# A transformer block on one core: its head with one-column matmuls, column arithmetic on ScalarE, products ordered by pass

## The chip, the cores and the metric

The kernel runs on one core of a Trainium2 chip. Times are device microseconds (us) of one execution. The profile records one execution; its times count from the start of its span.

## The reference

One block of a transformer, for 256 tokens (S) of 1024 features (D), in float32. A vector `c` sets six columns of modulation. What matters here is the first part, up to the projection; all that follows (attention of 8 heads, a gating unit, a feed-forward of width 4096, a last norm) is the same before and after.

```
c_act = jax.nn.silu(c)
mod = (c_act @ w_ada[l] + b_ada[l])[:, None, :]
shift1, scale1, gate1, shift2, scale2, gate2 = jnp.split(mod, N_MOD, axis=-1)
h = rmsnorm(x, g_mix[l]) * (1 + scale1) + shift1
proj = h @ w_in[l]
q, k, v, u, vs, ga, gb = jnp.split(proj, splits, axis=-1)
...
x = x + gate2 * (jnp.square(jax.nn.relu(h @ w_ff1[l])) @ w_ff2[l])
return rmsnorm(x, g_final)
```

## The kernel before

Features lie on partitions, tokens in the row. Every product of two float32 matrices is made from three passes of `float32r`: an operand is split into a high part (a copy cast to `float32r`) and a low part (the rest), and the passes are high by high, high by low and low by high. For weights, ScalarE (ACT) makes the high part `whi`, and VectorE (DVE) the low part `wlo`. Weights come in chunks of 1 MB (`raw`, five buffers) through the queue of SyncE (SP), in the order in which they are used.

**The head** loads the constants and x, makes silu(c) and spreads it over all partitions (`cps` by eight matmuls with an identity matrix, copied to `csb`), squares x, adds the squares up on VectorE, and sums them over the features by two matmuls with one column of ones. GpSimd (POOL) raises the sums to the power of -0.5 (`rs`); two matmuls spread that over the partitions (`rp`), and x times it is `xn`. Its first feature tile is multiplied on VectorE, the seven others on GpSimd. A few matmuls on a tile of zeros (`idle`, the function `spin`) are put in between.

**Phase 1** is a loop `kt` over the eight tiles of 128 features of h. A step has one chunk of adaLN weights and one of the projection. VectorE takes two products with `csb` along the row (`dot`, written `junk` in the trace, 1024 elements each, with a sum that a read of the accumulator delivers), makes from them the columns `acol` (scale) and `bcol` (shift), then `hf` = acol * xn + bcol. ScalarE makes the same with rounding, `hh`; VectorE takes the difference, `hl`. Then TensorE (PE) runs 24 products of 256 columns (q and k) and 12 of 512 columns (v and vs) on the step, into eight banks that are summed over all eight steps.

The orders on TensorE, VectorE and ScalarE in head and phase 1 are those in which the code is written (`InOrder`, pinned). In a step, ScalarE's casts `w_hi` are written around `h_hi`, so that one half of a step's weights is cast ahead of its `hh`. After phase 1 a scheduler orders the instructions.

Of the kernel before, what the change touches and what calls it, by code (L numbers as in the profile page):

```python
# [16 lines left out]
P = 128  # L17
# [17 lines left out]
class InOrder:  # L35
    """An engine whose instructions are issued in the order in which they are traced."""
# [11 lines left out]
def block_kernel(ctx, tc, xT, cols, wsguT, bsgu, w_a1, w_1, w_a, w_m, w_f, out):  # L48
# [46 lines left out]
    DVE.memset(ones, 1.0)  # L95
    nhalf = const.tile([P, 2], F32, name="nhalf")
    DVE.memset(nhalf, -0.5)
# [10 lines left out]
    eps = const.tile([P, 1], F32, name="eps")  # L108
    DVE.memset(eps, EPS)

    def sums(o, sq, first, last):
# [4 lines left out]
    def rstd(o, n):  # L116
        ms = wk.tile([P, 2], F32, name="ms", tag="ms")
        ACT.activation(out=ms, in_=o[:, 0:2], func=AF.Identity, scale=1.0 / n, bias=eps)
        rs = wk.tile([P, 2], F32, name="rs", tag="rs")
        nc.gpsimd.tensor_tensor(out=rs, in0=ms, in1=nhalf, op=ALU.pow)  # L120
        return rs

    def spread(rs):
        """One value per token, tokens on partitions -> on every partition, tokens in the row."""
        rp = bank()
        for t in range(2):
            PE.matmul(out=rp[:, P * t:P * t + P], lhsT=rs[:, t:t + 1].broadcast_to([P, P]), rhs=ident,
                      start=t == 0, stop=True, skip_group_check=t == 1)
        return rp

# [1 line left out]
    c_col = cols_sb[:, C_COL:C_COL + KT]  # L132
    cs = const.tile([P, KT], F32, name="cs")
    ACT.activation(out=cs, in_=c_col, func=AF.Tanh, scale=0.5)
    DVE.scalar_tensor_tensor(out=cs, in0=cs, scalar=1.0, in1=c_col, op0=ALU.add, op1=ALU.mult)
    csb = const.tile([P, D], F32, name="csb")
# [5 lines left out]
    ss = bank()  # L142
    sqs = [act.tile([P, 2, S], F32, name="sq", tag=t) for t in ("q1", "q2", "o1", "o2")]
    for i in range(4):
        ACT.activation(out=sqs[i], in_=x_sb[:, 2 * i:2 * i + 2], func=AF.Square)
        if i:
            DVE.tensor_tensor(out=sqs[0], in0=sqs[0], in1=sqs[i], op=ALU.add)
    DVE.tensor_tensor(out=sqs[0][:, 0], in0=sqs[0][:, 0], in1=sqs[0][:, 1], op=ALU.add)
    sums(ss, sqs[0][:, 0], True, True)
    for i in range(2):  # L150
        ACT.copy(out=csb[:, 512 * i:512 * i + 512], in_=cps[i])
    spin(4)
    rs1 = rstd(ss, D)
    identb = const.tile([P, P], BF16, name="identb")
    mask = const.tile([P, 2, P], BF16, name="mask")

# [17 lines left out]
    def column(acc, part, kt):  # L174
# [3 lines left out]
        if part in (SCALE1, SCALE2):  # L178
            g = (G_MIX, G_FFN)[n]
            DVE.scalar_tensor_tensor(out=acol[:, n, at], in0=acc, scalar=cols_sb[:, g + kt:g + kt + 1],  # L180
                                     in1=pre[:, n, at], op0=ALU.mult, op1=ALU.add)
        elif part in (SHIFT1, SHIFT2):
            DVE.tensor_tensor(out=bcol[:, n, at], in0=acc, in1=b, op=ALU.add)
# [4 lines left out]
    # the middle's weight chunks, and the adaLN chunks that are used beside them  # L188
# [62 lines left out]
    hh = act.tile([P, KT, S], F32R, name="hh", tag="b1")  # L251
    hl = act.tile([P, KT, S], F32R, name="hl", tag="b2")
    rb1 = wk.tile([P, S], F32, name="rb1", tag="sqa", bufs=1)
    xn = act.tile([P, KT, S + 2], F32, name="xn", tag="b3")
    wsg = const.tile([P, 8, P], F32, name="wsg", tag="c4")
    bsg = const.tile([P, NP, P], F32, name="bsg")
    for kt in range(KT):
        if kt + 2 < KT:
            ada[kt + 2] = load(w_a1[kt + 2], 2 if kt + 2 == KT - 1 else 1)
            wraw[kt + 2] = load(w_1[kt + 2], 4 if kt + 2 == KT - 1 else 2)  # L260
        raw, w_raw = ada.pop(kt), wraw.pop(kt)
# [4 lines left out]
        wp = [slice(2048 // np_ * i, 2048 // np_ * (i + 1)) for i in range(np_)]  # L266

        def w_hi(i):
# [5 lines left out]
        def cols_ab():  # L274
            column(da, SCALE1, kt)
            column(db, SHIFT1, kt)

        def h_hi():
            a, b = acol[:, 0, kt:kt + 1], bcol[:, 0, kt:kt + 1]
            ACT.activation(out=hh[:, kt], in_=xn[:, kt, 0:S], func=AF.Identity, scale=a, bias=b)  # L280
            DVE.tensor_scalar(out=hf, in0=xn[:, kt, 0:S], scalar1=a, scalar2=b, op0=ALU.mult, op1=ALU.add)

        def h_lo():
            DVE.tensor_tensor(out=hl[:, kt], in0=hf, in1=hh[:, kt].bitcast(F32), op=ALU.subtract)

        da, db = dot(raw, 0), dot(raw, 1)
        if kt == 0:
            for i in range(3):
                w_hi(i)
            cols_ab()  # L290
            rp = spread(rs1)
            spin(4)
            DVE.tensor_tensor(out=xn[:, 0, 0:S], in0=x_sb[:, 0], in1=rp[:, 0:S], op=ALU.mult)
            h_hi()
            w_lo(0)
            ACT.copy(out=rb1, in_=rp[:, 0:S])
            for i in range(1, KT):
                nc.gpsimd.tensor_tensor(out=xn[:, i, 0:S], in0=x_sb[:, i], in1=rb1, op=ALU.mult)
            w_lo(1)
            h_lo()  # L300
            w_lo(2)
            w_hi(3)
            w_lo(3)
            qk_ps = [bank() for _ in range(4)]
            vv_ps = [[bank() for _ in range(2)] for _ in range(2)]
        else:
            w_hi(0)
            cols_ab()
            h_hi()
            w_lo(0)  # L310
            w_hi(1)
            h_lo()
# [4 lines left out]
        f, l = kt == 0, kt == KT - 1  # L317
        for ft in range(8):
            o = qk_ps[ft // 2][:, S * (ft % 2):S * (ft % 2) + S]
            w = slice(P * ft, P * ft + P)  # L320
            mm3(o, wh[:, w], wl[:, w], hh[:, kt], hl[:, kt], f and ft % 2 == 0, l,
                skip_group_check=ft % 2 == 1)
        for n in range(2):
            w = slice(1024 + 512 * n, 1536 + 512 * n)
            for t in range(2):
                tk = slice(P * t, P * t + P)
                o = vv_ps[n][t]
                PE.matmul(out=o, lhsT=hh[:, kt, tk], rhs=wh[:, w], start=f, stop=False)
                PE.matmul(out=o, lhsT=hl[:, kt, tk], rhs=wh[:, w], start=False, stop=False)
                PE.matmul(out=o, lhsT=hh[:, kt, tk], rhs=wl[:, w], start=False, stop=l)  # L330
# [36 lines left out]
    def wide(n, ah, al, nk, base=0):  # L367
        """Two tiles of features from one chunk, tokens in the row."""
# [46 lines left out]
    def attn_turn(pr):  # L415
        # transposed probabilities: [keys 0:128 x queries 0:256 | keys 128:256 x queries 128:256]
# [48 lines left out]
    A0, S0, TD, OD = 1, 5, 2, 3  # when attention and the gating unit start; lags of transposes and products  # L465
# [233 lines left out]
    for q, first, last in ((sq3[:, 0], True, False), (sq[:, 0], False, False), (sq[:, 1], False, True)):  # L699
        sums(ss3, q, first, last)  # L700
    for ft in range(4, KT):
        turn(ft)
    rs3 = rstd(ss3, D)
# [11 lines left out]
def _ko(w, cols):  # L715
    """[K, N] -> chunks [N/cols][128][K/128 * cols] with k in (ko, p)."""
# [42 lines left out]
```

## Time and profile before

| what | value |
|---|---|
| time, median of 3 runs | 376.34 us (376.22 to 376.67) |
| the profiled execution: span from first to last instruction | 374.8 us |
| TensorE busy | 358.4 us (96%), 2884 matmul records |
| VectorE busy | 266.4 us (71%) |
| ScalarE busy | 206.0 us (55%) |
| GpSimd busy | 15.4 us (4%) |
| moved by DMA | 89.34 MB, mean 238 GB/s |

The profiled execution has no separate time on record: its span is 374.8 us, and the median lies 1.5 us above it. A busy share is a mean over the span; what a change in the head is worth depends on which wait ends last there.

### The profile page before, as it was taken

Reading aid. Unit: us, or ns where it says so; the run is one execution under the profiler, and the core shown is the slowest. Engines: PE = TensorE matmul, PEld = TensorE weight load, DVE = VectorE, ACT = ScalarE, POOL = GpSimd, SP = SyncE. Lnnn points to the kernel's source line nnn. Section 1 sums busy time; section 2 is a strip of 40 time slices with the busy share of each in tenths; the row PEclk is TensorE's granted clock in tenths of the full one; section 3 lists DMA queues with packets and bytes.
Section 4 is the critical chain, followed back from the end, with each engine's and each line's share of the span. In section 5 each row is a group of like instructions: output and inputs, shape, how many; then the busy total and the mean of one; then the engine's idle time right before and its main releaser. Section 6 shows DMA issues by size and latency. Waiting matters only on the chain.

```text
span 374.8 us, 6928 instructions
## 1 busy us (share of the span) xinstructions
PE 358.4 (96%) x2884; PEld 346.5 (92%) x2884; DVE 266.4 (71%) x420; ACT 206.0 (55%) x283; POOL 15.4 (4%) x21
## 2 busy tenths in 40 slices
PE   4779999999999999999999999999999999999993
PEld 3469989999899999999999999999999999999993
DVE  2899997687989986899856755766656545546442
ACT  4424346999894374356566544655445645446242
POOL 1460000010000000000000000000000000000001
PEclk9999999999999999999999999999999999999997
DMA  7999999987789995467755494764856554500003
GB/s 246 410 348 346 346 348 398 320 321 259 269 309 357 353 396 226 152 232 282 251 210 189 150 334 147 299 231 150 299 202 257 217 201 147 215 1 2 2 0 112
DMA packets 16126, 89.34 MB, mean 238 GB/s; under 512 B 1888, under 2 KB 2400, under 8 KB 7136
## 3 DMA queue, kind: packets, MB, share of 16 engines
q1 hardware_dynamic: 16096, 88.92, 64.9%
q8 instruction: 22, 0.36, 0.4%
q14 instruction: 8, 0.07, 0.0%
HBM read 87.86 MB, written 1.05 MB: 237 GB/s over the span
## 4 chain that ended last, share of the span: by engine, by line
PE 92%; issue 3%; DVE 3%; POOL 1%; POOLq 0%; DVEq 0%; ACT 0%
PE bank L44 92%; DVE junk L44 1%; DVE wlo L44 1%; POOL rs L120 0%; DVE hl L44 0%; DVE ys L44 0%; POOLq L755 0%; DVEq L755 0%; DVE acol L44 0%; DVE xn L44 0%; POOL maskf L103 0%; DVE maskf L44 0%; DVE idle L44 0%; ACT ms L44 0%; DVE ones L44 0%
## 5 line engine op out<-in xcount | busy, mean ns | idle before, releaser
L44 ACT CAST whi<-raw 128x2048 fp32r<-128x2048 f32 (+2 forms) x74 | 112.6, 1537 | 79.3 <-PE bank L44 77.7
L44 DVE TENSOR_TENSOR wlo<-raw,whi 128x2048 fp32r<-128x2048 f32 (+2 forms) x74 | 135.8, 1842 | 9.1 <-ACT whi L44 7.9
L44 PE MATMUL bank<-zh,whi 128*128 128x258 f32 x256 | 72.5, 283 | 0.0
L44 PE MATMUL bank<-zh,wlo 128*128 128x258 f32 x256 | 72.3, 282 | 0.0
L44 PE MATMUL bank<-zl,whi 128*128 128x258 f32 x256 | 72.2, 282 | 0.0
L44 PE MATMUL bank<-fl,whi 128*128 128x256 f32 x256 | 72.0, 281 | 0.0
L44 PE MATMUL bank<-fh,wlo 128*128 128x256 f32 x256 | 71.9, 281 | 0.0
L44 PE MATMUL bank<-fh,whi 128*128 128x256 f32 x256 | 71.9, 281 | 0.0
L44 PE MATMUL bank<-hl,whi 128*128 128x256 f32 x224 | 63.5, 283 | 2.4 <-DVE hl L44 2.4
L44 PE MATMUL bank<-hh,whi 128*128 128x256 f32 x224 | 64.5, 288 | 1.2 <-ACT hh L44 1.2
L44 PE MATMUL bank<-hh,wlo 128*128 128x256 f32 x224 | 63.3, 282 | 0.0
L44 DVE SCALAR_TENSOR_TENSOR junk<-raw,csb 128x1024 bf16<-128x1024 f32 x48 | 58.4, 1239 | 0.0
L44 PEld LDWEIGHTS bank<-fh,whi 128*128 128x128 f32 x256 | 49.1, 192 | 0.0
L44 PEld LDWEIGHTS bank<-zl,whi 128*128 128x128 f32 x256 | 48.4, 189 | 0.0
L44 PEld LDWEIGHTS bank<-zh,whi 128*128 128x128 f32 x256 | 48.3, 189 | 0.0
L44 PEld LDWEIGHTS bank<-zh,wlo 128*128 128x128 f32 x256 | 48.3, 189 | 0.0
L44 PEld LDWEIGHTS bank<-fh,wlo 128*128 128x128 f32 x256 | 48.1, 188 | 0.0
L44 PEld LDWEIGHTS bank<-fl,whi 128*128 128x128 f32 x256 | 48.0, 188 | 0.0
L44 PEld LDWEIGHTS bank<-hh,whi 128*128 128x128 f32 x224 | 42.9, 192 | 3.2 <-ACT hh L44 2.0
L44 PEld LDWEIGHTS bank<-hl,whi 128*128 128x128 f32 x224 | 42.7, 191 | 3.3 <-DVE hl L44 2.9
L44 PEld LDWEIGHTS bank<-hh,wlo 128*128 128x128 f32 x224 | 42.8, 191 | 0.0
L44 DVE TENSOR_TENSOR fl<-r,fh 128x512 fp32r<-128x512 f32 x16 | 11.1, 694 | 30.2 <-PE bank L44 28.9
(132 smaller groups left out, 488.7 us busy)
## 6 DMA issues: line engine op xcount, KB each, us to landing
raw<-in_w_f SPq DMA_DIRECT2D x32, 1024.0 KB, 4.8
raw<-in_w_a SPq DMA_DIRECT2D x22, 1024.0 KB, 5.8
raw<-in_w_m SPq DMA_DIRECT2D x16, 1024.0 KB, 6.5
raw<-in_w SPq DMA_DIRECT2D x12, 512.0 KB, 6.6
raw<-in_w_a SPq DMA_DIRECT2D x4, 512.0 KB, 6.8
raw<-in_w SPq DMA_DIRECT2D x8, 256.0 KB, 7.2
x_sb<-in_xT SPq DMA_DIRECT2D x2, 512.0 KB, 5.2
raw<-in_w_m SPq DMA_DIRECT2D x4, 256.0 KB, 6.8
```

The lines of the kernel that those rows point to most:

```text
L44: return lambda *a, **k: pin(op(*a, **k))
```

## The change

The first step's two columns no longer come from VectorE. Their weights are stored the other way round (`w_a0`, features of c on partitions), and 16 matmuls of one column each, with `ch` = silu(c) in its column form, sum them into one bank (`first_cols`). The sums of squares of x go the same way: 16 matmuls of one column each, straight from the squares, with `ones` set to 1/1024, in place of the additions on VectorE and two such matmuls. Two of the four squares move to VectorE. x is loaded in four pieces. GpSimd makes only the power (once on constants ahead of time), no multiplies: VectorE multiplies the seven other tiles of `xn` in one instruction. `acol` and `bcol` of the scale and shift parts, and `hf`, are made by ScalarE. In each step TensorE goes through a piece of the weights pass by pass: all products of the first pass, then of the second, then of the third.

```
+    def power(ms):
+        rs = wk.tile([P, 2], F32, name="rs", tag="rs")
+        nc.gpsimd.tensor_tensor(out=rs, in0=ms, in1=nhalf, op=ALU.pow)
+        return rs
+
+    power(ones[:, 0:2])
...
+    for i in range(4):
+        xi = x_sb[:, 2 * i:2 * i + 2]
+        if i % 2:
+            DVE.tensor_tensor(out=sqs[i], in0=xi, in1=xi, op=ALU.mult)
+        else:
+            ACT.activation(out=sqs[i], in_=xi, func=AF.Square)
+        for j in range(2):
+            means(ss, sqs[i][:, j], i == 0 and j == 0, i == 3 and j == 1)
...
+    first_cols = bank()
+    for k in range(KT):
+        for i in range(2):
+            w = slice(256 * k + P * i, 256 * k + P * i + P)
+            PE.matmul(out=first_cols[:, i:i + 1], lhsT=ada0[:, w], rhs=ch[:, k:k + 1], start=k == 0 and i == 0,
+                      stop=k == KT - 1, skip_group_check=i == 1)
+    rp = spread(rs1)
+    DVE.tensor_tensor(out=xn[:, 0:1, 0:S], in0=x_sb[:, 0:1], in1=rp, op=ALU.mult)
+    spin(3)
...
-            DVE.scalar_tensor_tensor(out=acol[:, n, at], in0=acc, scalar=cols_sb[:, g + kt:g + kt + 1],
-                                     in1=pre[:, n, at], op0=ALU.mult, op1=ALU.add)
+            ACT.activation(out=acol[:, n, at], in_=acc, func=AF.Identity, scale=cols_sb[:, g + kt:g + kt + 1],
+                           bias=pre[:, n, at])
...
+        def split(i):
             ACT.copy(out=wh[:, wp[i]], in_=w_raw[:, wp[i]])
-
-        def w_lo(i):
             DVE.tensor_tensor(out=wl[:, wp[i]], in0=w_raw[:, wp[i]], in1=wh[:, wp[i]].bitcast(F32), op=ALU.subtract)
...
-            w_hi(0)
-            cols_ab()
-            h_hi()
-            w_lo(0)
-            w_hi(1)
-            h_lo()
-            for i in range(1, np_):
-                w_lo(i)
-                if i + 1 < np_:
-                    w_hi(i + 1)
...
+        column(da, SCALE1, kt)
+        column(db, SHIFT1, kt)
+        a, b = acol[:, 0, kt:kt + 1], bcol[:, 0, kt:kt + 1]
+        ACT.activation(out=hh[:, kt], in_=xn[:, kt, 0:S], func=AF.Identity, scale=a, bias=b)
+        ACT.activation(out=hf, in_=xn[:, kt, 0:S], func=AF.Identity, scale=a, bias=b)
+        if not f:
+            split(0)
+        DVE.tensor_tensor(out=hl[:, kt], in0=hf, in1=hh[:, kt].bitcast(F32), op=ALU.subtract)
+        for i in range(0 if f else 1, np_):
+            split(i)
+        if f:
+            DVE.tensor_tensor(out=xn[:, 1:KT, 0:S], in0=x_sb[:, 1:KT], in1=rp.broadcast_to([P, KT - 1, S]),
+                              op=ALU.mult)
...
+        for i in range(np_):
+            lo, hi = wp[i].start, wp[i].stop
+            for p, (w_, h_) in enumerate(((wh, hh), (wh, hl), (wl, hh))):
+                for ft in range(lo // P, min(hi, 1024) // P):
...
```

The order on ScalarE in two steps of the middle of phase 1, before (`whi<-raw` is a cast of half a chunk, the names in `hh<-xn,bcol,acol` are those of the text above):

```order
L44 CAST whi<-raw 128x1024 [waits DMAHW2_49]
L44 ACTIVATE hh<-xn,bcol,acol 128x256 [waits DVE_49,Pool_49]
L44 CAST whi<-raw 128x1024 [waits DMAHW3_49]
L44 CAST whi<-raw 128x1024 [waits DMAHW5_49]
L44 ACTIVATE hh<-xn,bcol,acol 128x256 [waits DVE_49,Pool_49]
L44 CAST whi<-raw 128x1024 [waits DMAHW6_49]
```

And the same place with the change, from the columns of step 1 to the casts of step 2:

```order
L44 ACTIVATE acol<-acc,pre,cols_sb 128x1 [waits DVE_49]
L44 ACTIVATE bcol<-acc,cols_sb 128x1 [waits DVE_49]
L44 ACTIVATE hh<-xn,bcol,acol 128x256 [waits Activation_49]
L44 ACTIVATE hf<-xn,bcol,acol 128x256
L44 CAST whi<-raw 128x1024 [waits DMAHW6_49]
L44 CAST whi<-raw 128x1024 [waits DMAHW7_49]
L44 ACTIVATE acol<-acc,pre,cols_sb 128x1 [waits DVE_49]
L44 ACTIVATE bcol<-acc,cols_sb 128x1 [waits DVE_49]
L44 ACTIVATE hh<-xn,bcol,acol 128x256 [waits Activation_49]
L44 ACTIVATE hf<-xn,bcol,acol 128x256
L44 CAST whi<-raw 128x1024 [waits DMAHW1_49]
L44 CAST whi<-raw 128x1024 [waits DMAHW2_49]
```

Before, the first cast of a step stood ahead of its `hh`; now both casts stand behind the columns, `hh` and `hf` of their own step.

On VectorE the rows of steps 1 and 2 with the change:

```order
L44 SCALAR_TENSOR_TENSOR junk,acc<-raw,csb 128x1024 [waits DMAHW5_49]
L44 SCALAR_TENSOR_TENSOR junk,acc<-raw,csb 128x1024
L44 TENSOR_TENSOR wlo<-raw,whi 128x1024 [waits DMAHW6_49,Activation_49]
L44 TENSOR_TENSOR hl<-hf,hh 128x256
L44 TENSOR_TENSOR wlo<-raw,whi 128x1024 [waits DMAHW7_49,Activation_49]
L44 SCALAR_TENSOR_TENSOR junk,acc<-raw,csb 128x1024 [waits DMAHW0_49,DVE_49]
L44 SCALAR_TENSOR_TENSOR junk,acc<-raw,csb 128x1024 [waits DVE_49]
L44 TENSOR_TENSOR wlo<-raw,whi 128x1024 [waits DMAHW1_49,Activation_49]
```

`acol`, `bcol` and `hf`, which stood between the products and `wlo` before, are gone from VectorE; the next step's products stand behind the second `wlo` as before.

On TensorE the start of the program with the change (`ones,sq` are the sums of squares, `ch,raw` the first columns, `ident,rs` the spreading of the power):

```order
L44 MATMUL bank<-idle 128x512
L44 MATMUL bank<-ident,cs 128x128 x8
L44 MATMUL bank<-ones,sq 128x1 x16
L44 MATMUL bank<-ch,raw 128x1 x16
L44 MATMUL bank<-ident,rs 128x128 x2
```

Before, two `ones,sq` stood there and no `ch,raw`.

## Rows read from the trace of the kernel before

**Rows 1.** The page's busy times (engine, us, share, instructions).

```profile
PE 358.4 (96%) x2884; PEld 346.5 (92%) x2884; DVE 266.4 (71%) x420; ACT 206.0 (55%) x283; POOL 15.4 (4%) x21
```

**Rows 2.** The chain that ended last: start, us, what.

```profile
19.77 3.36 DVE junk L44 x4
...
26.07 341.85 PE bank L44 x2807
```

**Rows 3.** Timeline of TensorE, phase 1: start, us, instruction, [idle before <-releaser].

```profile
24.55 0.38 PE L44 MATMUL bank<-hh,whi 128*128 128x256 f32 x1 [1.23 <-ACT hh L44]
26.07 0.45 PE L44 MATMUL bank<-hl,whi 128*128 128x256 f32 x1 [1.14 <-DVE hl L44]
...
61.34 0.28 PE L44 MATMUL bank<-hh,whi 128*128 128x256 f32 x1
...
66.97 0.28 PE L44 MATMUL bank<-hh,whi 128*128 128x256 f32 x1
```

**Rows 4.** Stretches: length, busy PE, PEld, DVE, ACT, POOL; granted clock, DMA.

```profile
10.00:11.00 1.00, 0.91 (x5) 0.91 (x6) 1.00 (x5) 0.00 (x0) 0.00 (x0) 1.00 1.07 391
...
23.00:26.00 3.00, 0.70 (x3) 0.19 (x1) 2.89 (x8) 2.11 (x3) 1.39 (x2) 1.00 0.89 315
26.00:29.50 3.50, 3.43 (x16) 3.44 (x17) 3.50 (x8) 0.38 (x1) 0.00 (x0) 0.53 0.79 274
```

**Rows 5.** Timeline of VectorE, one step of phase 1.

```profile
38.31 1.22 DVE L44 SCALAR_TENSOR_TENSOR junk<-raw,csb 128x1024 bf16<-128x1024 f32 x1
...
39.45 1.22 DVE L44 SCALAR_TENSOR_TENSOR junk<-raw,csb 128x1024 bf16<-128x1024 f32 x1
40.59 0.08 DVE L44 DVE_READ_ACCUMULATOR junk<-raw,csb 128x1 f32 x1
...
40.73 0.15 DVE L44 TENSOR_TENSOR bcol<-acc,cols_sb 128x1 f32<-128x1 f32 x1
40.99 0.42 DVE L44 TENSOR_SCALAR hf<-xn,acol,bcol 128x256 f32<-128x256 f32 x1
41.31 1.22 DVE L44 TENSOR_TENSOR wlo<-raw,whi 128x1024 fp32r<-128x1024 f32 x1
42.45 0.42 DVE L44 TENSOR_TENSOR hl<-hf,hh 128x256 fp32r<-128x256 f32 x1
42.79 1.22 DVE L44 TENSOR_TENSOR wlo<-raw,whi 128x1024 fp32r<-128x1024 f32 x1
43.92 1.22 DVE L44 SCALAR_TENSOR_TENSOR junk<-raw,csb 128x1024 bf16<-128x1024 f32 x1
```

**Rows 6.** Timeline of ScalarE in the same step.

```profile
40.97 0.60 ACT L44 ACTIVATE hh<-xn,bcol,acol 128x256 fp32r<-128x256 f32 x1 [3.12 <-DVE bcol L44]
41.48 1.99 ACT L44 CAST whi<-raw 128x1024 fp32r<-128x1024 f32 x2
```

**Rows 7.** Timeline of the head, and of TensorE's weight loads at the end.

```profile
3.04 3.49 PEld L44 LDWEIGHTS bank<-ident,cs 128*128 128x128 f32 x16 [3.04 <-POOL maskf L103]
...
6.10 2.44 ACT L44 ACTIVATE sq<-x_sb 128x512 f32<-128x512 f32 x4 [3.37 <-DMA x_sb<-in_xT]
...
10.09 0.93 PEld L44 LDWEIGHTS bank<-ones,sq 128*128 128x128 f32 x4 [3.56 <-DVE sq L44]
...
13.29 1.22 PE L44 MATMUL bank<-ident,rs 128*128 128x128 f32 x4 [0.46 <-POOL rs L120]
...
14.55 0.42 DVE L44 TENSOR_TENSOR xn<-x_sb,bank 128x256 f32<-128x256 f32 x1 [1.66 <-PE bank L44]
...
366.85 0.97 PEld L44 LDWEIGHTS bank<-ones,sqt 128*128 128x128 f32 x8
```

**Rows 8.** Timeline: small instructions of ScalarE, quarter pieces of ScalarE and VectorE.

```profile
11.14 0.26 ACT L44 ACTIVATE ms<-bank,eps 128x2 f32<-128x2 f32 x1 [1.64 <-PE bank L44]
11.30 1.13 ACT L44 CAST whi<-raw 128x512 fp32r<-128x512 f32 x2
...
59.12 2.49 DVE L44 TENSOR_TENSOR wlo<-raw,whi 128x512 fp32r<-128x512 f32 x4
```

More of the change, by code (lines that the diff above doesn't have):

```diff
@@ L105, in block_kernel, with means @@
         fill=NEG, base=0, channel_multiplier=1)
-    eps = const.tile([P, 1], F32, name="eps")
-    DVE.memset(eps, EPS)
-    def sums(o, sq, first, last):
+    nhalf = const.tile([P, 2], F32, name="nhalf")
+    DVE.memset(nhalf, -0.5)
+    def power(ms):
[3 more added lines that the diff above has]
+    power(ones[:, 0:2])
+    def means(o, sq, first, last):
         for t in range(2):
@@ L114, in sums, with rstd @@
                       stop=last, skip_group_check=t == 1)
-    def rstd(o, n):
+    def rstd(o):
         ms = wk.tile([P, 2], F32, name="ms", tag="ms")
[L118 to L121, printed above, removed]
+        DVE.tensor_scalar(out=ms, in0=o[:, 0:2], scalar1=EPS, scalar2=None, op0=ALU.add)
+        return power(ms)
     def spread(rs):
@@ L141, in block_kernel @@
                   start=kt % 4 == 0, stop=True, skip_group_check=kt % 4 > 0)
[L142 to L155, printed above, removed]
     acol = const.tile([P, 2, KT], F32, name="acol")
@@ L165, in block_kernel @@
             op0=ALU.add, op1=ALU.mult)
+    ss = bank()
+    sqs = [act.tile([P, 2, S], F32, name="sq", tag=t) for t in ("q1", "q2", "o1", "o2")]
+    for i in range(4):
+        xi = x_sb[:, 2 * i:2 * i + 2]
[6 more added lines that the diff above has]
+    for i in range(2):
+        ACT.copy(out=csb[:, 512 * i:512 * i + 512], in_=cps[i])
+    rs1 = rstd(ss)
+    xn = act.tile([P, KT, S + 2], F32, name="xn", tag="b3")
+    identb = const.tile([P, P], BF16, name="identb")
+    mask = const.tile([P, 2, P], BF16, name="mask")
+    first_cols = bank()
+    for k in range(KT):
+        for i in range(2):
+            w = slice(256 * k + P * i, 256 * k + P * i + P)
[3 more added lines that the diff above has]
+    DVE.tensor_tensor(out=xn[:, 0:1, 0:S], in0=x_sb[:, 0:1], in1=rp, op=ALU.mult)
+    spin(3)
     def dot(raw, i):
@@ L266, in block_kernel @@
         wp = [slice(2048 // np_ * i, 2048 // np_ * (i + 1)) for i in range(np_)]
-        def w_hi(i):
+        f, l = kt == 0, kt == KT - 1
+        def split(i):
             ACT.copy(out=wh[:, wp[i]], in_=w_raw[:, wp[i]])
-        def w_lo(i):
             DVE.tensor_tensor(out=wl[:, wp[i]], in0=w_raw[:, wp[i]], in1=wh[:, wp[i]].bitcast(F32), op=ALU.subtract)
[L274 to L281, printed above, removed]
@@ L317, in block_kernel @@
[L317 to L330, printed above, removed]
+        for i in range(np_):
+            lo, hi = wp[i].start, wp[i].stop
+            for p, (w_, h_) in enumerate(((wh, hh), (wh, hl), (wl, hh))):
+                for ft in range(lo // P, min(hi, 1024) // P):
+                    o = qk_ps[ft // 2][:, S * (ft % 2):S * (ft % 2) + S]
+                    PE.matmul(out=o, lhsT=w_[:, P * ft:P * ft + P], rhs=h_[:, kt],
+                              start=f and p == 0 and ft % 2 == 0, stop=l and p == 2, skip_group_check=ft % 2 == 1)
+                for n in range(max(lo - 1024, 0) // 512, max(hi - 1024, 0) // 512):
+                    for t in range(2):
+                        PE.matmul(out=vv_ps[n][t], lhsT=h_[:, kt, P * t:P * t + P],
+                                  rhs=w_[:, 1024 + 512 * n:1536 + 512 * n], start=f and p == 0, stop=l and p == 2)
@@ L699, in block_kernel @@
     for q, first, last in ((sq3[:, 0], True, False), (sq[:, 0], False, False), (sq[:, 1], False, True)):
-        sums(ss3, q, first, last)
+        means(ss3, q, first, last)
     for ft in range(4, KT):
         turn(ft)
-    rs3 = rstd(ss3, D)
+    rs3 = rstd(ss3)
     ys = act.tile([P, 2, D], F32, name="ys", tag="b2")
```

66 lines of the change are left out of this document (24 added, 42 removed).

## Prediction

> **What bounds the kernel now.** I read the busy times first: TensorE is busy for 358.4 of the span's 374.8 us [rows 1]. The chain that ended last says where the other time went: from 26.07 us on it is TensorE alone for 341.85 us; ahead of that it runs through VectorE's adaLN products [rows 2]. So a microsecond that TensorE wins or loses in head or phase 1 is one at the end, as long as the later stages keep it fed, and what must be found is when TensorE leaves phase 1. In the trace that is 66.97 us, one step of 36 products after 61.34: a step costs TensorE 5.63 us [rows 3].
>
> Ahead of 26.07 TensorE waited for step 1's `hh` and `hl` [rows 3], was busy 0.70 of 3 us, and then ran at a granted clock of 0.53, nearly all of it at the lower level of 1.2 GHz [rows 4]. That is the loss that could be won back. What could be lost is seen in VectorE's step: from the first product at 38.31 to the next one's at 43.92 it takes 5.61 us without a gap of note [rows 5], as long as TensorE's own 5.63. ScalarE has slack: it stood 3.12 us until `bcol` came [rows 6], its own work being 2.5 us a step.
>
> **The change: phase 1.** From VectorE's step go `acol`, `bcol` and `hf`: from the end of the products at 40.59 to `wlo` at 41.31, 0.72 us. Its own work falls to 5.61 - 0.72 = 4.9 us. But the order changes what VectorE waits for. ScalarE's queue now reads columns, `hh`, `hf`, cast, cast, and the columns wait for VectorE's products; VectorE's queue reads product, product, `wlo`, and `wlo` waits for the cast. Before, the first cast stood ahead of `hh`, so that `wlo` found it done. Now each step is one ring through both engines, and nothing is queued on VectorE that could fill the wait: behind the waiting `wlo` stand `hl`, the second `wlo` and the next step's products, for which ScalarE waits in turn. I add the ring up from the start of a step's first product:
>
> Two products, 1.14 us apart, and the read of the accumulator: 2.28 + 0.08 = 2.36 [rows 5]. To ScalarE 0.09 (`bcol` ended at 40.88, `hh` began at 40.97 [rows 5, 6]): 2.45. `bcol` on ScalarE isn't in the trace; the nearest row is `ms`, two columns, 0.26 [rows 8]: 2.71. Its hand-over to `hh` on the same engine lies between nothing and that 0.09; I take 0.07: 2.78. `hh` and the next start are 0.51 apart [rows 6]: 3.29. `hf` on ScalarE, an operation with the operands of `hh`, another 0.51: 3.80. The first cast, 1.99 us for two that overlap a little, some 1.04 for one [rows 6]: 4.84. To VectorE about 0.05: 4.89. `wlo` 1.14, `hl` 0.34, `wlo` 1.13 [rows 5]: **7.50 us**.
>
> So the step is 7.5 us where TensorE needs 5.63, and TensorE stands for about 1.9 us in each. Bounds: hand-overs at nothing and `bcol` at 0.15 (its time on VectorE [rows 5]) give 7.2; hand-overs at 0.15 each and `bcol` at 0.4 give 7.8. The order by pass asks for `hl` eight products later and `wlo` sixteen later than `hh`; it shortens the waits within a step, but can't beat the ring. If D is the start of step 1's first product, step 7's is at D + 6 x 7.5 = D + 45.0. In step 7 the pieces are quarters, so the first cast ends at 3.80 + 0.62 = 4.42 and TensorE starts at 4.45. Two products of a later chunk that the scheduler puts ahead of `wlo` (2.28 us) end at 4.64 and so hide in the wait, provided their weights are in. `wlo` 0.60 [rows 8] and `hl` 0.42 follow, to 5.66; TensorE has then done its first four products (0.47) and has 5.16 of its 5.63 left: it leaves phase 1 at D + 45.0 + 5.70 + 5.16 = D + 55.86. The difference to 66.97 is **D - 11.1**.
>
> **The change: the head.** `cps` waits for `cs` as before, and its 16 weight loads (each float32 matmul is two records) run at 0.21 us from one to the next from 3.04 on [rows 7]: done by 6.4. The three matmuls on zeros stand in the empty time ahead of it. Then come 32 matmuls of one column, 64 records. Such a record takes about 0.2 in the head (four in 0.93) and 0.11 near the end of the kernel (eight in 0.97) [rows 7]. The granted clock reads 1.00 in the head, but its loads are as slow there as in the 1.2 GHz stretch (17 in 3.44 us) [rows 4], so I go by the durations. At 0.21 the 64 take 13.4 us, to 19.9; at 0.11 they take 7.1, to 13.6. x is no bound: the four squares ended at 8.54 when ScalarE did them alone [rows 7], and two engines share them now. GpSimd's power runs beside the first columns. From spread to `xn` 1.26 us [rows 7], `xn` 0.42, the hand-over to `hh` as before: at the slow rate `hh` begins at 21.6, `hf` ends at 22.7. `hl` 0.34, four `wlo` of 0.60 [rows 8], then the seven tiles of `xn` in one instruction: 0.42 for 256 columns [rows 7], 0.69 for 512 (the last of four `wlo` at a distance of 0.60 that end 2.49 after the first's start [rows 8]), so 0.27 for each further tile, 2.0 in all. The four casts between, 0.51 apart [rows 8], keep ahead of `wlo`. That gives **D = 27.6** at the slow rate and, with a spread of 0.8, 20.9 at the fast one. (Before, the same product began at 19.77 [rows 2].)
>
> Which rate? In the head of before, 3.5 us of unbroken float32 matmuls of 128 columns (3.04 to 6.5) did not end the slow rate: the one-column records at 10.09 are still slow [rows 7]. They are the nearest rows to the new matmuls in kind and place, so I take the slow rate. The Trainium skill ("TensorE: Matmul & The Clock Gate", Part 1) says that the half clock is the default and that matmul activity releases it; it speaks for the fast rate somewhere in this unbroken run of 13 us, and that is the first rival below.
>
> The sum: 27.6 - 11.1 = 16.5 us more. The last sum of squares moves from ScalarE to VectorE for its small addition, 0.1 at most; I count it as nothing. DMA has to move 2.1 MB in a step of 7.5 us, 280 GB/s, and moved 315 and 391 in two stretches [rows 4]; it is no bound. Span 374.8 + 16.5 = 391.3; the median lies 1.5 above the span: **392.8 us**.
>
> **The rivals.**
>
> *The clock rises during the one-column matmuls.* For it: TensorE is without a gap from 3 us on. Against it: the rows at 10.09. D is then between 20.9 (from the start) and, with the means slow to 13.2 and the columns at 0.11, about 24; 9.8 to 13 more, 386 to 389, say 387.5.
>
> *The clock falls in the waits of each step.* It fell when TensorE was busy 0.70 of 3 us [rows 4]. With 1.9 idle in 7.5 it is busier than that. A slow stretch costs about 1.55 us (16 records in 3.43 us [rows 4], where 16 of 256 columns need 1.9 at 0.117 each, as 24 of these and 12 of twice the columns make up the 5.63 of [rows 3]); 5.63 + 1.55 is 7.2, hidden in the 7.5 of the ring except in the last step: 394.4.
>
> *The ring does not bind, and it is faster.* If ScalarE had the casts done ahead of the columns, VectorE would need 4.9 us a step, TensorE's 5.63 would bind, and with the fast rate in the head step 1's `hh` would come at 20.9 + 3.4 = 24.3; TensorE then leaves phase 1 at 24.4 + 0.5 + 7 x 5.63 = 64.3 or, with the clock rising late, a little later: 64.3 to 66; some 1 to 2.7 less, 374.5. It decides from a step of below 7.5 - 9.8/6 = 5.9 us on. Against it: the order of rows on ScalarE, and that ScalarE stood 3.12 us behind `hh` [rows 6] with a half of the next step's weights still to cast. The Trainium skill ("TensorE: Matmul & The Clock Gate", "Engine queue depths") calls ScalarE and VectorE strict FIFO queues, which speaks against this rival too.
>
> *Hardly anything changes:* the ring near 5.9 with the fast head, where loss and gain meet: 376.3.
>
> **How the numbers follow.** Forecast 0.55, clock rising in the head 0.29, clock falling in the steps 0.08, faster 0.05, no change 0.03. The three slower cases hold 0.92; faster by over 0.2% (0.75 us, about what a measurement tells from no change) 0.05, within 0.03. The range takes in the ring's bounds (6 x 0.3 = 1.8 either way) around the forecast and reaches down into the first rival: 385.5 to 395.
>
> **What the profile would show.** VectorE in phase 1 with a gap of 2.5 us ahead of each first `wlo`, put down to ScalarE's `whi`, and a period of 7.5 us; TensorE with two waits a step, some 1.2 for `hh`/`whi` and 0.7 for `hl`; one-column loads at 0.2 in the head; phase 1 left at about 83.5. I am wrong if the period is below 7.2, if the one-column records run at 0.11, or if a later stage takes the time back, which TensorE's share of 96% leaves no room for.

## The result and the profile after

The changed kernel takes 394.96 us (median of 4 runs, 392.65 to 395.58) where the kernel before takes 376.5 (376.22 to 376.99): a ratio of 1.0476, interval 1.0444 to 1.0508. The profiled execution took 395.48 us, with a span of 393.6.

The page after, busy times and granted clock in 40 slices:

```profile
span 393.6 us, 7024 instructions
PE 375.2 (95%) x2941; PEld 361.1 (92%) x2942; DVE 256.7 (65%) x378; ACT 216.9 (55%) x317; POOL 6.4 (2%) x15
PEclk9578999879999999999999999999999999999998
```

TensorE's busy time grew by 16.8 us [rows 1]. Its work is the same but for the one-column matmuls, whose 64 records fill 10.6 us here (6.74 to 17.29 us, below) where four took 1.0 before; the rest, some 7 us, was not taken apart, but matmuls at half clock are in it. The clock line shows where the half clock lies: in the first 35 us and near 80 us.

One step of VectorE in phase 1, against [rows 5]:

```profile
39.70 1.22 DVE L44 SCALAR_TENSOR_TENSOR junk<-raw,csb 128x1024 bf16<-128x1024 f32 x1
...
44.49 1.23 DVE L44 TENSOR_TENSOR wlo<-raw,whi 128x1024 fp32r<-128x1024 f32 x1 [2.42 <-ACT whi L44]
45.63 0.42 DVE L44 TENSOR_TENSOR hl<-hf,hh 128x256 fp32r<-128x256 f32 x1
45.97 1.22 DVE L44 TENSOR_TENSOR wlo<-raw,whi 128x1024 fp32r<-128x1024 f32 x1
47.10 1.22 DVE L44 SCALAR_TENSOR_TENSOR junk<-raw,csb 128x1024 bf16<-128x1024 f32 x1
```

ScalarE in the same step, against [rows 6]:

```profile
40.95 0.39 ACT L44 ACTIVATE acol<-acc,pre,cols_sb 128x1 f32<-128x1 f32 x1 [2.95 <-DVE junk L44]
42.10 0.29 ACT L44 ACTIVATE bcol<-acc,cols_sb 128x1 f32<-128x1 f32 x1 [0.75 <-DVE junk L44]
42.43 0.60 ACT L44 ACTIVATE hh<-xn,bcol,acol 128x256 fp32r<-128x256 f32 x1
42.93 0.59 ACT L44 ACTIVATE hf<-xn,bcol,acol 128x256 f32<-128x256 f32 x1
43.43 1.98 ACT L44 CAST whi<-raw 128x1024 fp32r<-128x1024 f32 x2
```

Each engine waits for the other once in a step: VectorE 2.42 us for the cast, ScalarE 2.95 us for the first product. The step is 47.10 - 39.70 = 7.40 us; it was 5.61. TensorE's waits, by what released them (us, times, longest), and the two of one step:

```profile
PE bank L44 <- ACT whi L44: 6.2, 7, 1.4
PE bank L44 <- DVE hl L44: 4.5, 6, 2.6
```

```profile
31.29 1.93 PE L44 MATMUL bank<-hl,whi 128*128 128x256 f32 x8 [0.38 <-DVE hl L44]
...
44.51 1.22 PE L44 MATMUL bank<-hh,whi 128*128 128x256 f32 x8 [0.86 <-ACT whi L44]
46.10 1.21 PE L44 MATMUL bank<-hl,whi 128*128 128x256 f32 x8 [0.37 <-DVE hl L44]
```

The first of these rows is step 1's: eight matmuls in 1.93 us, where step 3's take 1.21. That is the half clock again (the fourth slice of the clock line), and the ring hides it: step 1 is as long as the others.

The head on TensorE, against [rows 7], and stretches of it (length, busy PE, granted clock, DMA):

```profile
3.19 3.76 PE L44 MATMUL bank<-ident,cs 128*128 128x128 f32 x16 [0.47 <-DVE cs L44]
6.74 4.04 PE L44 MATMUL bank<-ones,sq 128*128 128x1 f32 x32
10.64 6.65 PE L44 MATMUL bank<-ch,raw 128*128 128x1 f32 x32
17.15 1.20 PE L44 MATMUL bank<-ident,rs 128*128 128x128 f32 x4
...
20.55 1.22 PE L44 MATMUL bank<-hh,whi 128*128 128x256 f32 x4 [0.92 <-ACT whi L44]
```

```profile
7.00:10.00 3.00, 3.00 (x26) 1.00 0.87 306
10.00:11.00 1.00, 1.00 (x11) 1.00 1.06 408
11.00:17.00 6.00, 6.00 (x31) 0.50 1.04 419
17.00:24.00 7.00, 5.86 (x24) 0.50 0.84 341
76.00:82.00 6.00, 4.98 (x22) 0.50 0.98 356
```

The records of the means take 0.126 us each, those of the columns 0.208: the rate rose in the first run and fell back at 11.0, with no gap in TensorE's records from 6.74 to 18 us.

The last step of phase 1, where VectorE, then TensorE wait:

```profile
73.65 1.23 DVE L44 SCALAR_TENSOR_TENSOR junk<-raw,csb 128x1024 bf16<-128x1024 f32 x1 [1.95 <-DMA raw<-in_w_a]
...
75.95 0.69 DVE L44 TENSOR_TENSOR wlo<-raw,whi 128x512 fp32r<-128x512 f32 x1
```

```profile
77.02 1.22 PE L44 MATMUL bank<-hl,whi 128*128 128x256 f32 x4 [2.57 <-DVE hl L44]
78.04 1.05 PE L44 MATMUL bank<-hh,wlo 128*128 128x256 f32 x4
...
82.95 0.63 PE L44 MATMUL bank<-wlo,hh 128*128 128x512 f32 x2
...
84.81 0.28 PE L44 MATMUL bank<-hh,whi 128*128 128x256 f32 x1
```

VectorE's product at 73.65 belongs to a later chunk; its weights were late by 1.95 us, `wlo` and `hl` of step 7 stand behind it, TensorE stood 2.57 us for `hl`, and its matmuls then ran at the lower level, 1.05 us for four that take 0.64 at the upper one.

All profiled executions in one table. D is the start of step 1's first product on VectorE; then the six steps to step 7's first product; from there to TensorE's first matmul behind phase 1; that matmul's start; and what is left of the span behind it. (Before, the product of D starts at 19.70; the chain of [rows 2] enters it at 19.77.)

```text
kernel     D     6 steps  last    left    rest    span
before   19.70   35.46   11.81   66.97   307.8   374.8
after    24.88   44.45   15.48   84.81   308.8   393.6
e1       24.90   35.66    9.62   70.18   309.2   379.4
e2       20.44   44.45   11.22   76.11   309.5   385.6
e3       18.66   42.66   10.52   71.84   307.9   379.7
e4       28.00   44.46   10.71   83.17   313.2   396.4
e5       20.27   35.66   10.00   65.93   309.0   374.9
e6       20.26   32.05   10.84   63.15   309.6   372.7
e7       18.55   32.28   12.12   62.95   309.3   372.2
e8       26.79   44.45   11.46   82.70   309.3   392.0
e9       25.91   44.47   13.01   83.39   309.5   392.9
e10      27.70   40.75   10.12   78.57   308.9   387.5
e11      26.09   44.81   11.80   82.70   310.8   393.5
e12      19.29   32.27   12.80   64.36   309.2   373.6
```

Of the 18.8 us that the span grew, the start took 5.2, the six steps 9.0, the last step 3.7 and all that follows 1.0. The profiled executions of e4 and e10 are the longest of their four, 398.11 and 389.34 us against medians of 395.6 and 386.37; their D of 28.00 and 27.70 belongs to such executions (the last section comes back to it).

### The profile page after: what moved, and what is told of

It reads as the page before. It is cut to its first block, busy times and chain, and to the rows that moved or that the text cites. A ratio compares the mean times of both kernels' runs of the same rounds, so it can differ in the third digit from the quotient of the medians.

```text
span 393.6 us, 7024 instructions
## 1 busy us (share of the span) xinstructions
PE 375.2 (95%) x2941; PEld 361.1 (92%) x2942; DVE 256.7 (65%) x378; ACT 216.9 (55%) x317; POOL 6.4 (2%) x15
## 3 DMA queue, kind: packets, MB, share of 16 engines
HBM read 87.86 MB, written 1.05 MB: 226 GB/s over the span
## 4 chain that ended last, share of the span: by engine, by line
PE 81%; DVE 7%; issue 3%; ACT 3%; DMA 3%; DVEq 0%; POOLq 0%; POOL 0%; ACTq 0%
PE bank L44 81%; DVE junk L44 4%; DMA raw<-in_w_a 2%; DVE wlo L44 2%; ACT whi L44 1%; ACT hf L44 1%; ACT hh L44 1%; DVE xn L44 1%; DMA cols_sb<-in_cols 0%; ACT bcol L44 0%; DVE x_sb L44 0%; DVE hl L44 0%; DVE ys L44 0%; POOLq L749 0%; POOL sq L675 0%
## 5 line engine op out<-in xcount | busy, mean ns | idle before, releaser
L44 DVE TENSOR_TENSOR wlo<-raw,whi 128x2048 fp32r<-128x2048 f32 (+2 forms) x74 | 134.3, 1825 | 29.5 <-ACT whi L44 20.0
L44 PE MATMUL bank<-hh,whi 128*128 128x256 f32 x224 | 57.1, 296 | 6.2 <-ACT whi L44 6.2
L44 PE MATMUL bank<-hl,whi 128*128 128x256 f32 x224 | 57.3, 298 | 4.5 <-DVE hl L44 4.5
L44 DVE SCALAR_TENSOR_TENSOR junk<-raw,csb 128x1024 bf16<-128x1024 f32 x46 | 55.0, 1217 | 4.1 <-ACT acol L44 2.1
L44 PE MATMUL bank<-hh,wlo 128*128 128x256 f32 x224 | 56.4, 294 | 0.0
L44 PEld LDWEIGHTS bank<-hh,whi 128*128 128x128 f32 x224 | 39.7, 196 | 10.7 <-ACT whi L44 9.7
L44 PEld LDWEIGHTS bank<-hl,whi 128*128 128x128 f32 x224 | 40.6, 202 | 5.9 <-DVE hl L44 5.9
L44 PEld LDWEIGHTS bank<-hh,wlo 128*128 128x128 f32 x224 | 40.5, 201 | 0.0
```

The costliest lines, as they stand in the source:

```text
L44: return lambda *a, **k: pin(op(*a, **k))
```

## The experiments

**e1: the first cast ahead of the columns.** Two theories stand against each other: the ring of VectorE and ScalarE makes the loss, or TensorE's head does.

```diff
+        if not f:
+            hi(0)
         column(da, SCALE1, kt)
         column(db, SHIFT1, kt)
...
-            split(0)
+            lo(0)
```

> The kernel after, with one thing put back: in steps 1 to 7 the first cast of a step's weights stands on ScalarE ahead of the step's columns, as it did before; nothing is left out of the computation. Theory 1 (the ring of VectorE's products, ScalarE's columns, hh, hf and cast, and VectorE's wlo sets a step of 7.4 us): wlo finds its cast done, VectorE's period falls to its own 5 us until TensorE binds at 5.63, TensorE starts step 1 at about 28.3 and leaves phase 1 at 68 to 70; time 378 to 381. Theory 2 (the head's 32 one-column matmuls and what they delay are the main loss, the steps only follow): the steps stay where they are or TensorE waits elsewhere as long; time above 388.

Measured: 381.15 us, ratio 1.0139 (1.0116 to 1.0162). VectorE's step:

```profile
46.59 0.42 DVE L44 TENSOR_TENSOR hl<-hf,hh 128x256 fp32r<-128x256 f32 x1 [0.35 <-ACT hf L44]
47.52 1.23 DVE L44 TENSOR_TENSOR wlo<-raw,whi 128x1024 fp32r<-128x1024 f32 x1 [0.52 <-ACT whi L44]
48.67 1.22 DVE L44 SCALAR_TENSOR_TENSOR junk<-raw,csb 128x1024 bf16<-128x1024 f32 x1
```

The wait of 2.42 for the first cast is gone; 0.35 for `hf` and 0.52 for the second cast are left, and the steps are 5.94 us apart. One moved cast gives back 13.8 of the 18.5 us, which is theory 1, 0.15 us above its range; in the profiled executions 8.8 in the six steps and 5.9 in the last one. The 8.8 are the ring's. The 5.9 are not its alone: the two products of a later chunk, late in the changed kernel's last step, stand behind that step here (at 69.15). D did not move.

**e2: step 0's columns by VectorE's products,** as before the change, in place of the 16 one-column matmuls on weights.

```diff
-    first_cols = bank()
-    for k in range(KT): ... PE.matmul(out=first_cols[:, i:i + 1], lhsT=ada0[:, w], rhs=ch[:, k:k + 1], ...)
+    da0, db0 = dot(ada0, 0), dot(ada0, 1)
```

> The kernel after, with step 0's two columns made by two products on VectorE again (its weights in the old layout, the 16 one-column matmuls of the first columns gone); the rest of the change stays, the ring too. Theory 1: the first product of step 1 starts at about 19.7 in place of 24.9, the steps stay at 7.4 us, time 389 to 391. Theory 2: most of the 18.5 us come back, time 376 to 381.

Measured: 387.97 us, ratio 1.0341 (1.0296 to 1.0387); better than theory 1's 389 to 391 and far from theory 2. D fell by 4.4 us, and the steps stayed at 7.41. The rest of the gain lies in the last step: VectorE's two products of the later chunk stand there as in the changed kernel, but their weights were late by 0.21 us and not 1.95, and the step took 11.22 against 15.48.

**e3: the kernel before, its first cast behind `hh`,** the smallest edit that makes the ring.

```diff
-            w_hi(0)
             cols_ab()
             h_hi()
+            w_hi(0)
             w_lo(0)
```

> The kernel before, with one part of the change alone: in steps 1 to 7 the first cast stands behind hh on ScalarE. Theory 1: VectorE waits for it in each step, its step grows from 5.61 to about 6.9 us (products 2.28, columns 0.29, hh 0.6, cast 1.04, wlo, hl, wlo 2.6, hand-overs), TensorE's lag of some 3 us in phase 1 is used up first, phase 1 ends at about 73; time 381 to 384. Theory 2: nothing of the head is touched, time 376 to 377.5.

Measured: 382.31 us, ratio 1.017 (1.0145 to 1.0194). One cast moved by two places costs 6 us in the old kernel too. The step's first `wlo`, now with a wait that [rows 5] don't have:

```profile
38.14 1.22 DVE L44 TENSOR_TENSOR wlo<-raw,whi 128x1024 fp32r<-128x1024 f32 x1 [1.15 <-ACT whi L44]
```

The step from this row's first product at 33.90 to the next at 40.76 is 6.86 us: of the change's 7.41 - 5.61 = 1.80 us, the place of the cast makes 1.25.

**e4: the later chunk's products not early.** They keep their written place on VectorE, behind phase 1, and can't be put into the last step.

```diff
+        DVE.pinned = m == 0
...
         column(dot(raw, half), ...)
+        DVE.pinned = False
```

> The kernel after, with the two products of a later chunk, which the scheduler had put into step 7 ahead of wlo, held behind the orders of phase 1. In the profile after VectorE waited 1.95 us for that chunk's DMA there, TensorE stood 2.6 us for hl, and the granted clock fell to the lower level for some 5 us. Theory 1 with that as a cost of its own: wlo of step 7 starts about 2 us earlier and the clock may hold, time 391 to 393.5. Rival: TensorE stands as long for something else or the products cost the same later, time 394 to 396.

Measured: 395.6 us, ratio 1.054 (1.05 to 1.058): no gain, as the rival says, though the last step is shorter by 4.8 us (10.71). The table shows both sides: what follows phase 1 grew by 4.4. TensorE's waits there, and two stretches:

```profile
PE bank L44 <- ACT pr L44: 2.4, 2, 1.9
```

```profile
102.00:107.00 5.00, 2.59 (x21) 0.98 0.46 151
107.00:112.00 5.00, 5.00 (x31) 0.68 1.00 415
```

TensorE waited 2.4 us for `pr`, and then had the granted clock at 0.68 for 5 us, some 1.6 us of loss; together 4.0 of the 4.4. In the changed kernel TensorE has no such wait there. By the order of the trace the likely cause is the later chunk's products, three of which now stand between the softmax's reductions on VectorE (95.73 to 99.41); that was not tried by itself. What the last step won was lost behind it. (In this profiled execution, and in e10's, D is some 3 us late as well: the records of the means took 0.21 us.)

**e5: e1 and e2 together.**

> The changed kernel with two edits together: in steps 1 to 7 the first half's cast and the ring's order as in e1, and step 0's two columns by products on VectorE as in e2. Theory 1 (the ring of VectorE and ScalarE and the late start are two separate losses that add): step 1's products start at 20.4 us as in e2, the steps are 5.94 us apart as in e1, so phase 1 is left 45.3 us later (as in e1), at 65.7 against 66.97 before; the time is that of e1 less 4.5, 376.7 (375.5 to 378). Rival (the early start is swallowed by something that e1's late start hid, such as weights that come later than the engines ask): phase 1 left at 68 or later, 379 to 381.

Its diff is the two above. Measured: 376.71 us, ratio 1.0032 (1.0008 to 1.0057), within a tenth of a microsecond of the sum. Phase 1 is left at 65.93, 1.0 earlier than before the change, and the rest of the span takes 1.1 more: it cancels out.

**e6: all casts ahead of the columns,** on top of e5.

```diff
-        if not f:
-            hi(0)
+        for i in range(0 if f else np_):
+            hi(i)
```

> e5 with both halves' casts ahead of ScalarE's column arithmetic in steps 1 to 7. Theory 1 (e1's step of 5.94 us is a ring that is left: products 2.36, bcol 0.33, hh 0.51, hf 0.49, the second cast 1.03, VectorE's second low half 1.15): with that cast out of the ring it is 5.4 us, less than TensorE's own 5.63, so TensorE sets the step, 0.31 us less in each of six: 374.8 (374 to 376). Rival (TensorE itself takes 5.94 us when the products are ordered by pass): the step stays at 5.94 and the time is that of e5.

Measured: 374.61 us, ratio 0.9991 (0.9961 to 1.002). VectorE's products are now 5.34 us apart:

```profile
25.60 1.22 DVE L44 SCALAR_TENSOR_TENSOR junk<-raw,csb 128x1024 bf16<-128x1024 f32 x1
...
30.94 1.22 DVE L44 SCALAR_TENSOR_TENSOR junk<-raw,csb 128x1024 bf16<-128x1024 f32 x1
```

TensorE's first matmuls of a step are 35.02 - 29.39 = 5.63 apart, without a wait: TensorE sets the step again, as theory 1 says, and the order by pass costs it nothing.

**e7: x scaled tile by tile,** from a copy of the factor in SBUF, on top of e6.

```diff
+    def scaled(kt):
+        DVE.tensor_tensor(out=xn[:, kt:kt + 1, 0:S], in0=x_sb[:, kt:kt + 1], in1=rp if kt < 2 else rb, op=ALU.mult)
...
+            if not l:
+                scaled(kt + 1)
...
-            DVE.tensor_tensor(out=xn[:, 1:KT, 0:S], in0=x_sb[:, 1:KT], in1=rp.broadcast_to([P, KT - 1, S]), ...)
+            scaled(1)
+            ACT.copy(out=rb, in_=rp)
```

> e6 with the seven tiles of x scaled by 1/rms one at a time: tile 1 ahead of step 1's products, each later tile in the step before its own, from a copy of the factor in SBUF. Theory 1 (the one instruction of 2.01 us on VectorE is on the path to step 1's products, and the later steps have room for 0.34 us each): step 1's products start 1.6 us earlier, at 18.8; TensorE, which waited 1.0 us for step 1's weights in e2, gains that much and no more, since it is then busy with step 0: 373.8 (373 to 374.5). Rival (step 0 on TensorE, at its slow rate, already sets the start of step 1): the time of e6 within 0.3.

Measured: 374.21 us, ratio 0.9977 (0.9945 to 1.001). D came 1.7 us earlier, and phase 1 was left only 0.2 earlier: TensorE was still at step 0, at half clock until 20 us, so this is the rival's reason more than the theory's, though the time lies in the theory's range.

**e8: a wide matmul behind each pair of one-column matmuls,** in the changed kernel.

```diff
                       stop=k == KT - 1, skip_group_check=i == 1)
+        spin(1)
```

> The changed kernel with one 128x512 bf16 matmul that nothing uses behind each of the eight pairs of step 0's one-column matmuls. Theory 1 (it is the run of one-column matmuls that lets the granted clock fall to 0.50 at 11.0 us): the granted clock stays at 1.00 there, the one-column records take 0.126 us each as those of the means did and not 0.206, with the eight wide ones some 5.7 us for the run against 6.65, and step 0 goes at the full rate: step 1's products start at 23 to 24 against 24.88, and the time is 392 to 394.5. Rival (the clock falls there whatever lies between, or these records take 0.206 at either clock): the run takes 10 us, step 1's products start at 28, and the time is 397 to 399.

Measured: 393.88 us, ratio 1.048 (1.0437 to 1.0523). The time is in the range of theory 1, but not for its reason:

```profile
10.63 0.67 PE L44 MATMUL bank<-ch,raw 128*128 128x1 f32 x4
11.54 0.85 PE L44 MATMUL bank<-ch,raw 128*128 128x1 f32 x4 [0.24 <-issue]
12.25 0.59 PE L44 MATMUL bank<-idle 128*128 128x512 bf16 x1
```

```profile
7.00:11.00 4.00, 4.00 (x35) 1.00 1.02 337
11.00:21.00 10.00, 9.76 (x44) 0.50 0.97 384
22.00:26.00 4.00, 3.54 (x27) 1.00 0.57 188
```

The granted clock fell at 11.0 all the same and stayed at 0.50 for 10 us; D came 1.9 us later, behind the longer run. So the forecast of theory 1 failed on the clock. But the edited run starts at 10.63, only 0.4 us ahead of the fall, and the 32 one-column records of the means ahead of it were left as they were: whether such a run brings the fall is not shown either way. Step 0 did go at the full rate here (1.00 from 22.00 on), where in the changed kernel it was still at 0.50 until 24. The time is lower because the last step took 11.46 us and not 15.48: the later chunk's weights were late by 0.44 us there and not by 1.95, and the clock stayed up.

**e9: the products by tile again,** in the changed kernel.

```diff
-            for p, (w_, h_) in enumerate(((wh, hh), (wh, hl), (wl, hh))):
-                for ft in range(lo // P, min(hi, 1024) // P):
+            for ft in range(lo // P, min(hi, 1024) // P):
+                for p, (w_, h_) in enumerate(passes):
```

> The changed kernel with the three products of each tile next to each other again, as before the change, in place of all first, all second, all third products of a piece. Theory 1 (the order of the products costs and gains nothing while the ring of VectorE and ScalarE sets the step: TensorE has 7.41 - 5.63 = 1.8 us to spare in it, and by tile it stands longer at the step's first low part, some 0.9 us, out of that): the steps stay 7.4 us apart, and the time is 394 to 396. Rival (the order by pass costs TensorE something of its own, so that by tile is quicker): under 393. Other rival (the order by pass hides the wait for the low parts, and without it the step grows): over 398.

Measured: 394.59 us, ratio 1.0476 (1.0445 to 1.0507), as theory 1 says: the steps stay at 7.41, the wait for `hl` is 1.21 in a step and not 0.38, and the ring hides it.

**e10: the column arithmetic back on VectorE,** in the changed kernel.

```diff
-        ACT.activation(out=hf, in_=xn[:, kt, 0:S], func=AF.Identity, scale=a, bias=b)
+        DVE.tensor_scalar(out=hf, in0=xn[:, kt, 0:S], scalar1=a, scalar2=b, op0=ALU.mult, op1=ALU.add)
```

(and `acol`, `bcol` of phase 1 in their old form)

> The changed kernel with the column arithmetic (acol, bcol) and hf of the first phase back on VectorE, in the same order of the casts. Theory 1 (two things make the ring: the cast behind the columns, which e3 alone showed to give 6.86 us, and the three instructions moved to ScalarE, which add the rest, 0.55): the steps are 6.86 us apart, six of them 3.3 us less than 7.41; 391 to 392.5. Rival (the moved instructions are hidden behind the casts or VectorE needs the room for them): 394.5 to 396.

Measured: 386.37 us, ratio 1.0287 (1.0253 to 1.0321); 5 us better than expected. The steps are 6.79 apart, as forecast. What I had not seen is the last step: the later chunk's products no longer stand in it (they follow at 77.36), and it took 10.12 against 15.48.

**e11: the seven tiles scaled on GpSimd again,** in the changed kernel.

```diff
-            DVE.tensor_tensor(out=xn[:, 1:KT, 0:S], in0=x_sb[:, 1:KT], in1=rp.broadcast_to([P, KT - 1, S]), ...)
+            for i in range(1, KT):
+                nc.gpsimd.tensor_tensor(out=xn[:, i, 0:S], in0=x_sb[:, i], in1=rb, op=ALU.mult)
```

> The changed kernel with the seven tiles of x scaled on GpSimd again, from a copy of the factor in SBUF, as before the change. Theory 1 (it is an exchange: VectorE loses its 2.02 us instruction, but its wide instructions beside GpSimd take 1.75 us in place of 1.22, and so its four low parts of step 0 and two products of step 1 give most of it back): step 1's products start at 24 to 24.5 and end 26.5 to 27.5, against 27.17; 394 to 395.8. Rival (the 2.02 us come back whole): 392.5 to 393.3.

Measured: 395.65 us, ratio 1.0521 (1.0498 to 1.0544). It is an exchange, but no better one: VectorE's four `wlo` beside GpSimd took 4.64 us, not 2.50, and D came 1.2 later, not earlier.

**e12: e7 with the sums of squares by additions.**

```diff
+        if i:
+            DVE.tensor_tensor(out=sqs[0], in0=sqs[0], in1=sqs[i], op=ALU.add)
...
-        for j in range(2):
-            means(ss, sqs[i][:, j], i == 0 and j == 0, i == 3 and j == 1)
+    means(ss, sqs[0][:, 0], True, True)
```

> e7 with the sums of squares as before the change: four squares on ScalarE, four additions on VectorE, and two one-column matmuls in place of sixteen. Theory 1 (the run of one-column matmuls is what goes ahead of the fall of the granted clock at 10 to 11 us in all kernels that have it; before the change there was none and the clock stayed at 1.00 to 26 us): the granted clock stays at 1.00 through step 0, which TensorE then does in some 5.7 us and not 7.5; the first tile comes 0.7 us later (14.55 before the change against 13.83); step 1 begins on TensorE at 22.5 to 23 against 23.36; 373.4 to 374.1. Rival (the clock falls there without the run too): step 1 begins at 24 or later, 374.7 to 375.5.

Measured: 374.1 us, ratio 0.9948 (0.9929 to 0.9968), not to be told from e7's 374.21. The time is at the edge of theory 1's range; its forecast of the clock failed. Without the run of one-column matmuls the granted clock falls as well:

```profile
6.00:8.00 2.00, 0.08 (x1) 1.00 0.98 337
9.00:21.00 12.00, 7.94 (x31) 0.50 1.02 406
```

Here TensorE stood from 6.1 to 10.15, so idle time goes ahead of this fall, where in the changed kernel and in e8 there was none. The edit took the run away and put a wait in its place, and so it can't tell whether the run brings the fall in the kernels that have it. This kernel's interval lies below 1: it is the lowest median of the study, 0.5% under the kernel before. It has six executions, all of them within 375.3 us, where three of e7's twelve took 377.8 to 377.9; the medians are 0.1 us apart, so that its interval lies below 1 and e7's does not may be chance.

## Why the prediction was right, and where its sizes were off

**Slower, by the ring: right, and shown from both sides.** The step was 7.41 us where the prediction had 7.50, with 2.42 us of wait ahead of `wlo` (2.5 in the prediction), inside the bounds of 7.2 to 7.8 (the upper one's own terms add up to 7.88). Making the ring in the old kernel (e3) costs 6 us, opening it in the new one (e1) gives back 13.8, of which 8.8 lie in the six steps, opening it altogether (e6) puts the step back at TensorE's 5.63. e3 and e10 share out the 1.80 us: 1.2 for the cast's place, 0.6 for the three instructions that went to ScalarE. TensorE's two waits a step were sized a little high: 0.86 and 0.38 for 1.2 and 0.7.

**The start: the term D was mis-sized, 24.88 for 27.6.** The step that failed is the choice of the slow rate for all 64 one-column records. The first 32 took 0.126 us each, as the first rival had it, and so the prediction's own sign of being wrong, one-column records at the fast rate, was half met; the other 32 took 0.208, as the forecast had it. That rival's 24 for D is nearer than the forecast's 27.6, though it had the slow half first. The Trainium skill ("TensorE: Matmul & The Clock Gate", Part 1) says that activity releases the half clock and an idle stretch brings it back. The rise in the run of means agrees. The fall at 11.0 is not of that kind by the profile's records, which have no gap from 6.74 to 18 us in the changed kernel; what brought it stays open.

**The last step: mis-sized by 4.6, the largest error.** The prediction had 10.86 (5.70 + 5.16) and the trace has 15.48. The step that failed is "hide in the wait, provided their weights are in": the weights came 1.95 us late. The other 2.65 are the half clock behind TensorE's wait of 2.57 us: its matmuls ran at half rate from 77.02 to some 82.7. So the second rival's mechanism, the clock that falls in a wait, did happen here, and in step 1, behind a wait of 1.4, where the ring hid it as that rival says, but not in the waits of 0.9 and 0.4 us of steps 2 to 6. Its figure, 394.4, is the nearest to the measured 394.96, at a chance of 0.08; it priced the slow stretch at 1.55 and had no late weights. That the lateness and the clock are the cause and not the products themselves is seen in e2, where the same two products stand there with 0.21 us of wait (11.22), and in e4, where they are away (10.71). e9 parts the two: its weights were late by 1.67 us and TensorE stood 2.50 us for `hl`, but the clock stayed at 1.00, and the step took 13.01. So a wait of that length does not bring the fall every time. The products' transfer was issued at 64.32 and took 9.24 us in the changed kernel, 7.50 in e2. In these 9.24 us the DMA engines were busy 0.95 of the time, against 0.83 in the six steps ahead (32.28 to 69.33), so "it is no bound" held for the steps and not here. In e2's 7.50 us the share was 0.94 too; what made the one transfer longer was not tried.

**The rest: 1.0 us more, predicted as nothing.** In all kernels made from the changed one it takes 308.8 to 310.8 us (313.2 in e4), in the two of the old form 307.8 and 307.9. About three quarters of it lie between the first scores (`kT,qT`) and the output projection's products (`oh,whi`): these start 5.74 and 69.74 us behind phase 1 before, 5.78 and 70.53 after. Which instruction makes it was not tried, and stays open. It is why e6, which leaves phase 1 3.8 us before the old kernel, ends only 2.1 earlier.

The errors, -2.7 - 0.55 + 4.6 + 1.0, add up to the 2.3 us by which the span missed 391.3. That the time lies in the range is luck in part: the median of 394.96 is 0.04 us under its upper end, 395, and two of four executions are above it. Had D been the 27.6 of the sum and the rest as measured, the time would have been some 397.7. The range allowed for the ring's bounds and for a faster head, not for the last step. The parts of the change that were counted as nothing were so: the order by pass (e9), and, as an exchange, GpSimd's multiplies (e11).

## What to carry to other kernels

Moving work from a full engine to one with slack shortens nothing if it also puts that work between two things the full engine waits for: add up the ring, not the busy times, and put whatever needs no result of the ring (here the casts) ahead of it in the engine's order. When an instruction from a later stage is filled into a wait, ask when its data land, because all that stands behind it waits too. And a wait that is taken out of one stage by holding work back may come up again where that work then stands: e4 won 4.8 us in the last step and lost 4.4 behind it.

## What was not expected of the hardware

**The granted clock in the head.** A clock that reads 1.00 at the start of a span is no reading. The trace's entries of the granted clock begin with a rise, at 7.59 us in the changed kernel, 16.00 in the kernel before, 28.26 in e4 and 29.56 in e10, and where no entry stands yet the views count 1.00. The records are slow up to that entry and fast behind it: in e10 two 128x512 matmuls are 0.43 us apart at 28.66 and 0.24 from 30.00 on. So the head of the kernel before ran at the lower level until 16.00, as the prediction judged by the durations, against the 1.00 of [rows 4].

In every kernel that was profiled with a rise before 8 us, the clock fell to 0.50 between 8 and 11 us. Ahead of the fall TensorE stood idle in e3 and e12; in the others it ran the one-column matmuls of the means, or had just done so. The head of e3 is that of the kernel before, word for word, and its clock rose at 7.04 us: the same head comes out either way. What decides it, and whether the run of one-column matmuls brings the fall, was not found.

A high mean clock therefore does not mean a fast execution: of e6's twelve, the eight at 0.977 to 0.983 took 374.1 to 375.5 us and the four at 0.993 to 0.997 took 377.2 to 377.9. It is no rule either: e12's one execution at 0.996 took 374.6, within the range of its others.

**GpSimd's power of two columns** takes 0.70 us alone and 1.65 beside VectorE's products. The rows of the changed kernel and of e2:

```profile
11.05 0.70 POOL L112 TENSOR_TENSOR rs<-ms,nhalf 128x2 f32<-128x2 f32 x1 [8.30 <-DVE ms L44]
```

```profile
10.98 1.65 POOL L112 TENSOR_TENSOR rs<-ms,nhalf 128x2 f32<-128x2 f32 x1 [8.23 <-DVE ms L44]
```

In e2 VectorE's first product runs from 10.86 to 12.01 and the second follows at once; the power ends 0.62 us after the first one's end. The Trainium skill ("SBUF — State Buffer", "Who interferes with whom") says that a VectorE instruction with two SBUF inputs and a GpSimd instruction that reads SBUF contend for a shared port; these rows agree, and so does e11, where four `wlo` beside GpSimd's multiplies take 4.64 us and not 2.50.
